# The first modulations of a diffusion block: pages of w_ada laid out in 4 KB rows, and VectorE's share turned and summed in one instruction

## Chip, cores and metric

The kernel runs on one core of a Trainium2 chip. The metric is device microseconds for one execution; a measurement gives the median of several runs. The profile is one further execution, taken by the hardware profiler.

## The reference

One layer of a diffusion backbone over 1024 latent tokens and 256 context tokens, 1024 channels wide, everything in float32. A conditioning vector sets shift, scale and gate of every sublayer, and the context has a vector of its own:

```python
mods   = jnp.split(jax.nn.silu(c) @ w_ada[layer] + b_ada[layer], N_MOD, axis=-1)            # N_MOD = 9
mods_c = jnp.split(jax.nn.silu(c_ctx)[None] @ w_ada[layer] + b_ada[layer], N_MOD, axis=-1)
h  = ffn_sublayer(h,  mods[0],   mods[1],   mods[2],   g_ffn1[layer], w_ffn1_in[layer], w_ffn1_out[layer])
hc = ffn_sublayer(hc, mods_c[0], mods_c[1], mods_c[2], g_ffn1[layer], w_ffn1_in[layer], w_ffn1_out[layer])
# ffn_sublayer: hn = rmsnorm(h, g) * (1 + scale) + shift; a, b = split(hn @ w_in); h + 0.5 * gate * ((silu(a) * b) @ w_out)
```

Behind it come a mixing layer, a second such sublayer and a norm. Only the first two modulations (m = 0, the shift, and m = 1, the scale) bear on the change: 2 x 1024 columns of w_ada, each a sum over 1024 channels, for two vectors (q = 0 for c, q = 1 for c_ctx).

## The kernel before

Channels lie on partitions, tokens on the free axis, so a modulation vector is a tile of 128 partitions by 8 blocks (index d). Products of weights run in float32 split into a high and a low float32r part: `split` copies the high part on ScalarE (L145) and subtracts it on VectorE (L146), and `mm3` (L182) multiplies high by high, high by low and low by high.

The kernel begins with the context's first feed-forward layer. Its input `hnc` needs the norm of the context and the modulations 0 and 1 for c_ctx. Their 2048 columns of w_ada are cut into four quarters of 256 columns (qt 0 to 3; two blocks d of both m). Quarters 0, 1 and 3 go to TensorE: `ada_page` (L844) loads a page of two channel blocks, each by a transfer of 256 KB whose rows are two pieces of 1 KB; `ada_rows` (L850) multiplies it with silu(c) and silu(c_ctx) as two stationary columns, so that the sums lie along the free axis of two partitions; `ada_copy` (L854) takes them to SBUF, `ada_flip` (L859) turns them onto partitions, and `ada_done` (L879, L887) adds the bias and makes the scale. Quarter 2 goes to VectorE: `side` multiplies and adds each page into two accumulators (L791, L793), `ada_red` transposes and reduces them (L797, L798), and `ada_side` adds the four groups of partitions through a product (L867) and eight small adds (L871).

`nct` is the context's norm: squares on ScalarE (L205, L208) and their sum on VectorE (L209), `rstd` (sums on TensorE L214, a short chain on VectorE, a diagonal L224, L225), `bcast` (L230), `scaled0` (L938). `mod0(d, ...)` makes blocks of hnc: an activation with scale and bias (L931) and a cast (L932) on ScalarE, the low part on POOL for even d and on VectorE for odd d (L934). `idle` runs small products on `junk` (L922).

TensorE, VectorE and ScalarE run in exactly the order in which this part is written, up to the end of the first weight pair (f = 0). In that pair the products of the first six channel blocks come first; `last0`, called inside it, flips quarter 3, makes blocks 6 and 7 of hnc and loads the third weight tile. All loads are issued by SP, in order. `W.load` brings a tile of w1i (512 KB, rows of 4 KB) and splits it. The page pool `hnp` has two tags, pg0 and pg1, of 8 slots of 4 KB each per partition; `fxpage` has 12.

## Time and profile before

| | |
|---|---|
| median of 3 runs | 2645.05 us (2644.9 to 2646.2) |
| the profiled execution | 2649.01 us, span 2647.2 us |
| TensorE busy | 2630.2 us, 99% of the span |
| VectorE busy | 1947.5 us, 74% |
| ScalarE busy | 1202.1 us, 45% |
| POOL busy | 75.3 us, 3% |
| bytes moved by DMA | 452.73 MB, mean 171 GB/s |

Busy time is what the profiler records for an engine's instructions. Matmuls are pipelined, so a busy TensorE is not one at its peak. A matmul of float32 operands shows as two passes. Times in the rows count from the span's start.

### The profile page before, as it was taken

The numbers are of one execution on the slowest core, as the hardware profiler recorded it, in microseconds if no ns is written. First come the engines' busy times: TensorE is split into PE (matmuls) and PEld (weight loads), VectorE is DVE, ScalarE is ACT, GpSimd is POOL, SyncE is SP. The second block draws the span as 40 slices with busy tenths as digits, with TensorE's granted clock in tenths as the row PEclk, the third lists the DMA queues.
The fourth block names the chain that finished last, engine by engine and source line by source line (L and its number), as shares of the span: only waits on it lengthen the run. The fifth ranks groups of instructions, "written<-read, shape, count | busy, mean of one in ns | idle before, by whom it ended". The sixth has DMA issues, their size and how long they took to land.

```text
span 2647.2 us, 35936 instructions
## 1 busy us (share of the span) xinstructions
PE 2630.2 (99%) x12904; PEld 2212.0 (84%) x12904; DVE 1947.5 (74%) x3490; ACT 1202.1 (45%) x2167; POOL 75.3 (3%) x158
## 2 busy tenths in 40 slices
PE   9999999999999999999999999999999999999998
PEld 6998888888889878888888888888888888888887
DVE  7988688687989646777674878777568766665855
ACT  5664444444347525564443454333256444344433
POOL 0000000000000000000000002221000000000000
PEclk9999999999999999999999999999999999999999
DMA  9833344368587122356653566547341333337644
GB/s 313 308 112 132 123 163 164 115 237 302 176 278 262 66 80 91 104 175 197 197 177 106 174 207 233 176 152 268 128 143 41 128 139 115 120 123 278 201 159 178
DMA packets 201234, 452.73 MB, mean 171 GB/s; under 512 B 20320, under 2 KB 54624, under 8 KB 201056
## 3 DMA queue, kind: packets, MB, share of 16 engines
q1 hardware_dynamic: 200624, 450.05, 50.2%
q8 instruction: 101, 1.65, 0.3%
q14 instruction: 77, 0.63, 0.1%
q10 hardware_dynamic: 432, 0.39, 0.0%
HBM read 329.11 MB, written 121.32 MB: 170 GB/s over the span
## 4 chain that ended last, share of the span: by engine, by line
PE 93%; DMA 3%; issue 2%; DVE 1%; ACT 1%; SPq 0%; POOL 0%; POOLq 0%; DVEq 0%; ACTq 0%
PE qa L411 18%; PE pq L1379 16%; PE po L535 14%; PE qb L411 14%; PE pt L1863 10%; PE pr L1298 6%; PE pa L182 2%; PE pc L1165 2%; PE pb L182 2%; PE pn L2018 2%; DMA adapg<-in_w_ada_dram 1%; PE pu L1699 1%; PE pkc L1358 1%; PE pn L2016 1%; PE pvc L1455 1%
## 5 line engine op out<-in xcount | busy, mean ns | idle before, releaser
L146 DVE TENSOR_TENSOR ring<-rawq,ring 128x512 fp32r<-128x512 f32 x408 | 281.0, 689 | 222.3 <-ACT ring L145 220.9
L535 PE MATMUL po<-gring,wring 128*128 128x512 f32 (+1 forms) x1896 | 423.5, 384 | 0.0
L535 PEld LDWEIGHTS po<-gring,wring 128*128 128x128 f32 x1896 | 349.4, 188 | 70.1
L145 ACT CAST ring<-rawq 128x512 fp32r<-128x512 f32 x408 | 253.5, 622 | 310.9 <-PE pq L1379 84.6
L411 PE MATMUL qa<-fc,ring 128*128 128x512 f32 x1056 | 252.3, 389 | 0.0
L411 PEld LDWEIGHTS qa<-fc,ring 128*128 128x128 f32 x1056 | 198.1, 188 | 41.5 <-DVE fc L146 0.4
L1379 PE MATMUL pq<-fc,ring 128*128 128x512 f32 x864 | 207.4, 392 | 1.8 <-DVE sg L1437 1.8
L145 ACT CAST wring<-rw 128x512 fp32r<-128x512 f32 x154 | 95.7, 623 | 219.3 <-PE po L535 191.2
L1379 PEld LDWEIGHTS pq<-fc,ring 128*128 128x128 f32 x864 | 161.4, 188 | 35.1 <-DVE sg L1437 2.2
L1863 PE MATMUL pt<-yp,ring 128*128 128x512 f32 x768 | 186.3, 396 | 0.0
L1863 PEld LDWEIGHTS pt<-yp,ring 128*128 128x128 f32 x768 | 144.2, 190 | 28.7
L146 DVE TENSOR_TENSOR wring<-rw,wring 128x512 fp32r<-128x512 f32 x154 | 105.7, 687 | 83.6 <-ACT wring L145 83.2
L1379 PE MATMUL pq<-fa,ring 128*128 128x512 f32 x576 | 141.9, 394 | 0.0
L1379 PE MATMUL pq<-fb,ring 128*128 128x512 f32 x576 | 136.8, 391 | 0.0
L411 PE MATMUL qa<-fa,ring 128*128 128x512 f32 x528 | 126.9, 390 | 0.0
L411 PE MATMUL qa<-fb,ring 128*128 128x512 f32 x528 | 126.5, 390 | 0.0
L411 PE MATMUL qb<-fb,ring 128*128 128x512 f32 x528 | 126.4, 389 | 0.0
L1379 PEld LDWEIGHTS pq<-fb,ring 128*128 128x128 f32 x576 | 107.5, 188 | 22.4 <-issue 0.2
L411 PE MATMUL qb<-fc,ring 128*128 128x512 f32 x528 | 126.2, 389 | 0.0
L411 PE MATMUL qb<-fa,ring 128*128 128x512 f32 x528 | 126.2, 389 | 0.0
L1379 PEld LDWEIGHTS pq<-fa,ring 128*128 128x128 f32 x576 | 106.9, 188 | 22.0 <-DVE ring L146 0.3
L793 DVE SCALAR_TENSOR_TENSOR adacc<-adapg,sc,adacc 128x512 f32<-128x512 f32 x154 | 111.9, 746 | 17.1 <-DMA adapg<-in_w_ada_dram 15.9
(366 smaller groups left out, 4641.3 us busy)
## 6 DMA issues: line engine op xcount, KB each, us to landing
adapg<-in_w_ada_dram SPq DMA_DIRECT2D x144, 256.0 KB, 3.6
fsp<-fhl SPq DMA_DIRECT2D x66, 512.0 KB, 2.7
gring<-fsp SPq DMA_DIRECT2D x66, 512.0 KB, 4.2
raw<-in_w1i_dram SPq DMA_DIRECT2D x44, 512.0 KB, 5.1
graw<-fsp SPq DMA_DIRECT2D x88, 256.0 KB, 3.4
rawq<-in_w1i_dram SPq DMA_DIRECT2D x38, 512.0 KB, 3.6
rawq<-in_w2i_dram SPq DMA_DIRECT2D x38, 512.0 KB, 3.5
fsp<-p SPq DMA_DIRECT2D x66, 256.0 KB, 2.1
```

Source lines behind the costliest of these rows:

```text
L145: hi = S.copy(hl[:, 0, :], src)
L146: return hi, V.tensor_sub(hl[:, 1, :], src, hl[:, 0, :].bitcast(F32))
L182: T.matmul(pt, x, y, start=first and i == 0, stop=i == n - 1, skip_group_check=True)
L411: T.matmul(pt, hl[:, x, sl], pages[p][k][:, y, :], start=first and i == 0, stop=i == 11, skip_group_check=not first)
L535: T.matmul(pt[:, cs], w[:, x, sl], g[:, y, cs], start=grp and kp == 0 and i == 0, stop=kp == NFP - 1 and i == 2, skip_group_check=not grp)
L793: eng.scalar_tensor_tensor(acc, pgt, sc2[:, q, k:k + 1], acc, ALU.mult, ALU.add)
L1165: T.matmul(pt, hl[d // 4][:, x, sl], g[:, y, :], start=f == 0 and d % 2 == 0 and i == 0, stop=f == NF - 1 and i == 2, skip_group_check=True)
L1298: T.matmul(self.pt[m], pg[:, x, sl], hl[:, y, :], start=first and k == 0 and i == 0, stop=k == 3 and i == 2, skip_group_check=not first)
L1358: T.matmul(self.cp[:, o:o + 256], hl[:, x, k * 128:(k + 1) * 128], hnc[kc][:, y, :], start=p == 1 and k == 0 and i == 0, stop=p in (2, 4) ...
L1379: T.matmul(pt, hl[:, x, k * 128:(k + 1) * 128], pg[k][:, y, :], start=first and k == 0 and i == 0, stop=k == 3 and i == 2, skip_group_chec ...
L1863: T.matmul(pt, hl[:, x, k * 128:(k + 1) * 128], pg[:, y, :], start=kh + k + i == 0, stop=kh == 1 and k == 3 and i == 2)
L2018: T.matmul(pn[:, 0:257], qi[:, c_, :], self.C[d][:, c_, :], start=False, stop=c_ == 1)
```

## The change

The first two modulations are cut into 16 units of one block d of one m. Eleven go to TensorE (four, four and three in the groups 0, 1 and 3), five to VectorE. TensorE's pages are laid out by the host so that a page is one transfer with rows of 4 KB (3 KB in group 3). VectorE's units are turned by the host: output channels on partitions, the 1024 input channels along the free axis. To multiply them, silu(c) and silu(c_ctx) are spread over all partitions (`spread`: 16 products on TensorE, four copies on ScalarE), and one instruction for each unit and vector, `tensor_tensor_reduce`, multiplies a page with the spread row and sums the 1024 products, beginning with the bias, straight into `mods`. The accumulators, transposes, reductions and the eight small adds go. The counts of `idle` change, hnc's pair 4, 5 is made ahead of pair 2, 3, and the rest of w_ada keeps its rows in an array of its own.

```diff
     def ada_load(page, m, hf, k):
         pgt = page()
-        o = m * 1024 + hf * 512
+        o = (m - 2) * 1024 + hf * 512
...
-    NQ = 4
-    QW = 1024 // NQ
-    QD = QW // 128
-    KP = 512 // QW
+    KP = 2
+    UNITS = {0: [(m, d) for m in range(2) for d in (0, 1)], 1: [(m, d) for m in range(2) for d in (2, 3)],
+             3: [(0, 6), (1, 6), (1, 7)]}
+    SIDE = [(0, 4), (1, 4), (0, 5), (1, 5), (0, 7)]
 
     def ada_page(qt, kp, tag):
-        pg = hnp.tile([128, KP, 2, QW], F32, name="adapg", tag=tag, bufs=8)
-        for i in range(KP):
-            src = a["w_ada"][kp * KP + i].rearrange("p (m c) -> p m c", m=9)[:, 0:2, qt * QW:(qt + 1) * QW]
-            nc.sync.dma_start(pg[:, i], src)
...
+        pg = hnp.tile([128, KP, len(UNITS[qt]) * 128], F32, name="adapg", tag=tag, bufs=8)
+        nc.sync.dma_start(pg.rearrange("p k c -> p (k c)"), a[f"w_ada{qt}"][kp])
...
+    def side_page(u):
+        pg = hnp.tile([128, 1024], F32, name="adaT", tag="pg0", bufs=8)
+        nc.sync.dma_start(pg, a["w_adaT"][u])
+        return pg
...
-    def ada_side(qt, reds):
...
-        for q, red in enumerate(reds):
-            T.matmul(p8[:, q * 16:q * 16 + 16], grp4, red[:, 0:16], start=True, stop=True)
-        for q in (1, 0):
-            for r in range(4):
-                sl = slice(32 * r, 32 * r + 32)
-                V.tensor_add(mods[sl, 0:2, q, cs],
-                             p8[sl, q * 16:q * 16 + 16].rearrange("p (m d r) -> p m d r", m=2, r=4)[:, :, :, r], bv[sl, 0:2, cs])
-            scale_mod(0, 1, q, "g_ffn1", cs)
...
         for q in (1, 0):
...
+            if qt == 3:
+                ab = ((slice(0, 2), 6, pc[:, q:q + 3:2]), (slice(1, 2), 7, pc[:, q + 4:q + 5]))
+                for ms, d, src in ab:
+                    V.tensor_add(mods[:, ms, q, d], src, bv[:, ms, d])
+                scale_mod(0, 1, q, "g_ffn1", slice(6, 8))
...
-    for qt, kp in ((2, 0), (0, 0), (0, 1), (2, 1), (0, 2), (0, 3), (2, 2), (1, 0), (1, 1), (2, 3), (1, 2), (1, 3),
-                   (3, 0), (3, 1), (3, 2), (3, 3)):
-        pgs[qt, kp] = ada_page(qt, kp, "pg1" if qt % 2 else "pg0")
-    idle(30)
...
+    for qt, kp in ((0, 0), (0, 1), (2, 0), (0, 2), (0, 3), (2, 1), (1, 0), (1, 1), (2, 2), (1, 2), (1, 3), (2, 3),
+                   (3, 0), (3, 1), (2, 4), (3, 2), (3, 3)):
...
+    scB = [fxpage("scB", F32, (128, 1024)) for _ in range(2)]
+    waste = fxpage("waste", F32, (128, 1024))
...
+    def spread():
+        for q in range(2):
+            for hf in range(2):
+                pt = sm_ps("psc")
+                for j in range(4):
+                    T.matmul(pt[:, j * 128:(j + 1) * 128], sc2[:, q, hf * 4 + j:hf * 4 + j + 1].to_broadcast([128, 128]), ident,
+                             start=True, stop=True)
+                yield lambda q=q, hf=hf, pt=pt: S.copy(scB[q][:, hf * 512:(hf + 1) * 512], pt)
+
+    def side(u, qs=(1, 0)):
+        m, d = SIDE[u]
+        for q in qs:
+            V.tensor_tensor_reduce(waste, adaT[u], scB[q], 1.0, vs_("b_ada")[:, m * 8 + d:m * 8 + d + 1], ALU.mult, ALU.add,
+                                   mods[:, m, q, d:d + 1])
+
+    idle(14)
+    copies = list(spread())
     for d in range(NKT):
         nct.sq(d)
-    side(0, pgs[2, 0])
+    for f in copies:
+        f()
+    idle(5)
     prs = {0: mm_ps("adr")}
     ada_rows(prs[0], pgs[0, 0], 0)
     nct.rstd()
-    ada_rows(prs[0], pgs[0, 1], 1)
-    idle(3)
-    side(1, pgs[2, 1])
-    ada_rows(prs[0], pgs[0, 2], 2)
+    for kp in (1, 2):
+        ada_rows(prs[0], pgs[0, kp], kp)
+    side(0)
     nct.bcast()
     ada_rows(prs[0], pgs[0, 3], 3)
-    row = ada_copy(prs[0])
     scaled0()
-    side(2, pgs[2, 2])
-    idle(4)
+    row = ada_copy(prs[0], 0)
+    prs[1] = mm_ps("adr")
+    ada_rows(prs[1], pgs[1, 0], 0)
+    side(1)
+    for q in (1, 0):
+        scale_mod(0, 1, q, "g_ffn1", slice(4, 5))
     pc = sm_ps("adc")
     ada_flip(pc, row)
     ada_done(0, pc)
     mod0(0, 1)
-    prs[1] = mm_ps("adr")
-    for kp in range(NKT // KP):
+    for kp in (1, 2, 3):
         ada_rows(prs[1], pgs[1, kp], kp)
-    row = ada_copy(prs[1])
-    side(3, pgs[2, 3])
-    reds = [cp.tile([128, 32], F32, name="adred", tag="adred", bufs=2) for _ in range(2)]
-    for acc, red in zip(sides, reds):
-        ada_red(acc, red, 0)
+    row = ada_copy(prs[1], 1)
+    side(2)
+    side(3)
+    for q in (1, 0):
+        scale_mod(0, 1, q, "g_ffn1", slice(5, 6))
+    mod0(4, 5)
     prs[3] = mm_ps("adr")
     ada_rows(prs[3], pgs[3, 0], 0)
     pc = sm_ps("adc")
     ada_flip(pc, row)
     ada_done(1, pc)
     mod0(2, 3)
-    ada_rows(prs[3], pgs[3, 1], 1)
-    ada_side(2, reds)
-    for kp in (2, 3):
+    side(4)
+    for kp in (1, 2, 3):
         ada_rows(prs[3], pgs[3, kp], kp)
     W.load()
-    mod0(4, 5)
-    row = ada_copy(prs[3])
+    row = ada_copy(prs[3], 3)
     W.load()
...
+    r["w_ada"] = np.ascontiguousarray(wada[:, 2048:]).reshape(8, 128, 7168)
+    unit = lambda m, d: wada[:, m * 1024 + d * 128:m * 1024 + d * 128 + 128]
...
+        r[f"w_ada{qt}"] = np.ascontiguousarray(w.reshape(4, 2, 128, -1).transpose(0, 2, 1, 3)).reshape(4, 128, -1)
+    r["w_adaT"] = np.ascontiguousarray(np.stack([unit(*u).T for u in ((0, 4), (1, 4), (0, 5), (1, 5), (0, 7))]))
```

## Rows read from the trace of the kernel before

**Rows 1.** Page, part 1: busy us, share of the span and instructions, by engine.
```profile
PE 2630.2 (99%) x12904; PEld 2212.0 (84%) x12904; DVE 1947.5 (74%) x3490; ACT 1202.1 (45%) x2167; POOL 75.3 (3%) x158
```

**Rows 2.** Stretches: length, busy (count) PE, PEld, DVE, ACT, POOL, clock, DMA, GB/s.
```profile
6.50:30.50 24.00, 23.38 (x95) 9.28 (x93) 20.19 (x52) 6.09 (x16) 0.73 (x1) 1.00 1.09 349
30.50:36.00 5.50, 5.50 (x22) 2.05 (x22) 3.48 (x17) 3.38 (x6) 0.72 (x1) 1.00 1.04 400
...
45.30:175.00 129.70, 129.70 (x1052) 128.27 (x1053) 117.83 (x178) 87.06 (x127) 0.00 (x0) 1.00 0.74 258
```

**Rows 3.** Tile adapg up to 60 us: issues on SP, and issue to landing.
```profile
L844 SPq DMA_DIRECT2D adapg<-in_w_ada_dram x32: 367/368/1020, 2.7 to 27.3; - x32
...
DMA to landing us min/median/max: 6.0/6.0/7.6
```

**Rows 4.** Order of time, VectorE (DVE), 10 to 46 us: start, length, instruction.
```profile
15.71 2.73 DVE L793 SCALAR_TENSOR_TENSOR adacc<-adapg,sc,adacc 128x512 f32<-128x512 f32 x4
18.36 2.73 DVE L938 TENSOR_TENSOR hc<-hc,rb 128x256 f32<-128x256 f32 x8
21.00 2.73 DVE L793 SCALAR_TENSOR_TENSOR adacc<-adapg,sc,adacc 128x512 f32<-128x512 f32 x4
23.66 0.15 DVE L879 TENSOR_TENSOR mods<-adc,vec 128x4 f32<-128x4 f32 x1
...
26.11 0.42 DVE L934 TENSOR_TENSOR hnc<-nt,hnc 128x256 fp32r<-128x256 f32 x1 [1.84 <-ACT hnc L932]
26.45 2.73 DVE L793 SCALAR_TENSOR_TENSOR adacc<-adapg,sc,adacc 128x512 f32<-128x512 f32 x4
...
31.78 0.15 DVE L879 TENSOR_TENSOR mods<-adc,vec 128x4 f32<-128x4 f32 x1
...
34.17 0.42 DVE L934 TENSOR_TENSOR hnc<-nt,hnc 128x256 fp32r<-128x256 f32 x1 [1.77 <-ACT hnc L932]
...
36.19 1.23 DVE L146 TENSOR_TENSOR hl<-raw,hl 128x1024 fp32r<-128x1024 f32 x1
```

**Rows 5.** Order of time, TensorE (PE), 0 to 50 us.
```profile
10.05 1.88 PE L850 MATMUL adr<-adapg,sc 128*2 128x512 f32 x4 [0.36 <-DMA adapg<-in_w_ada_dram]
11.86 0.61 PE L214 MATMUL p<-ones,acc 128*128 128x1 f32 x4
...
33.63 3.60 PE L850 MATMUL adr<-adapg,sc 128*2 128x512 f32 x8
37.16 2.49 PE L182 MATMUL pa<-hnc,hl 128*128 128x256 f32 x18
39.58 1.05 PE L859 MATMUL adc<-cst,adrow 2*128 2x2 f32 x8
```

**Rows 6.** Stretch of the junk matmuls (L922) alone: PE busy and passes.
```profile
4.70:9.40 4.70, 4.70 (x44) 4.70 (x43) 1.00 1.08 357
```

**Rows 7.** Order of time, ScalarE (ACT), 5 to 46 us.
```profile
14.71 0.69 ACT L224 ACTIVATE diag<-cst,rs_y 128x128 fp32r<-128x128 f32 x2 [5.70 <-DVE rs_y L770]
...
25.04 0.60 ACT L931 ACTIVATE nt<-hc,mods,smod 128x256 f32<-128x256 f32 x1
```

**Rows 8.** Groups by form, VectorE, whole span: count, busy us, mean ns.
```profile
L1468 DVE SCALAR_TENSOR_TENSOR cv<-pre,vec,cv 128x1023 f32<-128x1023 f32 x16 | 20.4, 1278 | 0.9 <-ACT cv L1467 0.9
...
L791 DVE TENSOR_SCALAR adacc<-adapg,sc 128x512 f32<-128x512 f32 x22 | 10.2, 479 | 0.0
...
L225 DVE SCALAR_TENSOR_TENSOR diag<-cst,rs_y,diag 128x128 fp32r<-128x128 f32 x32 | 9.6, 348 | 1.4 <-ACT diag L224 1.4
...
L1592 DVE TENSOR_TENSOR_SCAN bcz<-R,bcz 128x128 f32<-128x128 f32 x1 | 0.4, 426 | 0.1
```

**Rows 9.** Stretches around a gap of TensorE, columns as in rows 2.
```profile
1581.30:1583.90 2.60, 0.00 (x0) 0.00 (x0) 2.60 (x5) 2.60 (x6) 2.55 (x6) 1.00 0.88 280
...
1585.00:1588.50 3.50, 3.50 (x11) 2.82 (x10) 3.50 (x7) 2.02 (x5) 0.00 (x0) 0.51 1.01 361
1588.50:1592.00 3.50, 3.50 (x17) 2.85 (x17) 2.96 (x7) 2.22 (x5) 0.00 (x0) 1.00 1.01 350
```

## The prediction

> **What bounds the kernel now.** I read the page first: TensorE is busy for 99% of the span [rows 1]. The change lies wholly ahead of the first weight products, so next come the stretches by time: from 45.3 to 175 us TensorE works without a gap [rows 2]. The stretch before that is a lead-in, and a microsecond saved or lost at its end moves everything behind it by a microsecond, because TensorE has no slack later with which to make it good. The measure of the change is therefore when TensorE enters steady work, about 45.3 us now.

> Inside the lead-in two things run side by side. The pages of w_ada stream from about 6.5 to 30.5 us at 349 GB/s, and as soon as tiles with 4 KB rows follow, the rate is 400 GB/s [rows 2]. The last page is issued at 27.3 us and takes about 6.0 us to land, so 33.3 us [rows 3]. VectorE meanwhile goes through one list in program order [rows 4]: four passes of multiply-add (two at 15.71 to 21.00 and so on), the scaling of the context by its norm, the adds that finish each quarter's modulations, and every second low part of hnc. The low part of W's first tile ends that list at 36.19 + 1.23 = 37.42 us. TensorE's row products end just then: its last eight begin at 33.63 and the first product of the weights at 37.16 [rows 5]. So at 37.4 us three chains arrive almost together: pages, TensorE's rows, VectorE's list. A change that shortens two of them gains nothing if the third gets longer.

> **The pages.** The bytes stay the same: 16 units of 128 columns by 1024 rows, 8.39 MB. At 349 GB/s they take 24.0 us, at 400 GB/s 21.0 us [rows 2]: the last page lands 3 us earlier, near 30.3 us. SP issues 17 transfers where it issued 32, and is nowhere last. The ninth page of the pg0 group must wait until TensorE has read the first one, at 10.65 + 1.88 = 12.5 us [rows 5], before its turn comes; no transfer queues behind it for that.

> **TensorE's own list.** Out go 36 of the 74 junk passes, the 4 small products of p8 and a quarter of each of the 16 passes of the last rows (384 columns for 512). In come 32 passes of 128 columns that spread silu(c). A pass of that shape takes 4.7/44 = 0.11 us [rows 6]. Ahead of the first rows stand 28 + 32 + 10 = 70 such passes instead of 60, so they end 10 x 0.11 = 1.1 us later. The old ones were over at about 9.5 us, and the old rows then stood waiting for their page until 10.05 [rows 5]; the new rows can begin at 9.5 + 1.1 = 10.65, with their page there: +0.6 us. The norm's sums move from 11.86 to 12.46 us [rows 5], and with them all that VectorE does after them. From there: sums 0.61, 28 row passes at (37.16 - 33.63)/8 = 0.44, the broadcast's two passes at 0.14 (2.49/18, also of 256 columns), 16 passes of three quarters at 0.33, two flips at 1.05 [rows 5]: 12.46 + 0.61 + 12.32 + 0.28 + 5.28 + 2.10 = 33.1 us. The new list of TensorE is done 4 us earlier than before, and the last page, wanted at 31.8 us, is there. If the pages came no faster, the last would hold these rows until about 34.6 us, which, as the next part shows, would also cost nothing.

> **ScalarE's copies.** Four copies of 128x512 out of PSUM come in behind the squares. ScalarE takes 0.60 us for 256 columns, so at most 1.2 each and 4.8 for the four, and it sat idle for 5.70 us before 14.71 [rows 7]: hidden. Without that idle time they would delay the norm, and through it the list below, by up to 4.8 us.

> **VectorE's blocks.** Ten instructions of 1024 elements replace sixteen of 512, two transposes, two reductions and eight adds of 32 partitions. No such multiply-and-sum is in the trace. The nearest row has two f32 inputs, a pointer scalar and 1023 elements: 1.278 us [rows 8]. Below it bounds the one-input form, 0.479 us for 512 [rows 8], about 0.75 for 1024; two tensors are read here, and no two-input f32 row comes near that. Above it bounds the scan: 0.426 us for 128x128 where the ordinary form takes 0.348 [rows 8]; if those 0.078 us go with the elements, 1024 of them cost 0.62 more, 1.90 us. I take 1.28, and 1.30 from one to the next, because all ten write the same scratch page.

> Now the list, step by step, old times from [rows 4]. The first pair begins at 15.71 + 0.60 = 16.31 and ends at 18.91. The scaling takes 2.64 (18.36 to 21.00): 21.55. Second pair: 24.15. Two small scale steps, 0.15 as the row at 23.66 and the hand-over, 0.18 each: 24.51. The adds of the first quarter begin there (before: 23.66, now +0.85), and the first low part begins 2.45 later as before (23.66 to 26.11), since VectorE waits for ScalarE: 26.96, done at 27.30. Two more pairs, 5.20: 32.50. Here the order changes: hnc's pair 4, 5 stands ahead of pair 2, 3. ScalarE gets its scale about 0.28 us later, at 32.78, and needs 1.07 (25.04 to VectorE's 26.11) [rows 4, 7]: 33.85. VectorE stands idle for this, with everything behind it: the adds of the next quarter, the last pair of blocks, W's splits. (POOL's half of pair 4, 5 is issued earlier too, and has until 40 us; W's raw tile, behind the pages in SP's queue, lands 3 us earlier than it did and waits.) Low part: 34.19. Adds and wait for pair 2, 3, as before 31.78 to 34.17, 2.39: 36.58, done 36.92. Last pair of blocks: 39.52. Then W's first split, which began at 36.19: **+3.3 us**. The removed transposes, reductions and adds are in this sum already, since they stood where the last pairs stand now. What is late next: the third product of the weights needs that low part, so TensorE, ready at 33.1, does two products when ScalarE's cast is there (about 37.7 us) and then waits until 40.75. Behind it lie the flip of the last quarter (6 passes for 8, 1.05/8 each, -0.26) and an add more before its scale (+0.1), and so ScalarE's last pair, W's third tile and steady work: **+3.2 us** in sum.

> **TensorE's clock.** TensorE now has a hole of about 4.6 us and one of 2.8 us. [...] On the chain stand 16 products after the wait, at 2.49/18 = 0.14 us, 2.2 us, and the flip. Bounds: nothing, if the clock is back by 40.75; 2.6 us, if all of it runs at half. By the row's ratio, 2.2 x (17/11 - 1) = **+1.2 us**, which I take.

> Sum: 3.2 + 1.2 = +4.4 us. On the profiled execution's own time, 2649.01 us, that is 2653.4. The median of the runs, 2645.05, lies 4.0 us lower, a difference that I let stand as that of a profiled run; from it the forecast is **2649.4 us**. A measurement can tell about 0.2%, 5.3 us, from no change, so this counts as no change, on the slow side.

> **The rivals.** *A block costs two instructions* (slower). If the sum comes out through a second, short instruction, each block grows by about the smallest VectorE row, 0.15 us [rows 4]: ten times, all on the chain, +1.5: 2650.9. It is decided at 5.3 us: (5.3 - 4.4)/10 = 0.09 us per block, so from 1.39 us a block on the kernel is measurably slower. The margin is small. Nothing in the trace speaks for or against it. [...]

> *A block runs at the scan's pace* (slower): ten times 0.62, +6.2 us over the forecast, 2655.6. Only its likeness to a scan speaks for it, and the row has 128 elements alone, so the excess may as well be a fixed 0.08 us.

> *VectorE isn't last* (faster side). If a block takes only 0.75 us, the list shortens by 5.3 us, W's split begins at 34.2, the hole for the clock is gone: 3.2 - 5.3 = -2.1, 2643.0. With blocks for nothing, TensorE's 33.1 against 37.16 caps the gain at 4.1 us, 2641: the lead-in alone can't give a measurable gain.

> *The rest moves.* The scratch pages are free again before their slots are wanted, and the later reads of w_ada keep rows of 2 KB; a shifted order of transfers later on could add or take some microseconds either way.

> **Chances.** Forecast (block 1.2 to 1.39 us) 0.55, of which 0.06 beyond 5.3 us through the clock; two instructions 0.19, of which 0.13 beyond it; scan's pace 0.06; VectorE not last 0.16; the rest 0.04, half of it each way. Slower 0.06 + 0.13 + 0.06 + 0.02 = 0.27; faster 0.03 (the rest, and a hundredth of the fourth); no change 0.70. The range takes in the fast rival and the two-instruction one with the clock's upper bound (+1.4), and leaves out the scan: 2642.5 to 2652.5 us.

> **What would show it.** Right: pages done by about 30.5 us with the rate near 400; TensorE's rows over at 33 us and a hole behind them; blocks at 1.28 us; W's first split beginning at 39.5 us; a granted clock under 1.00 near 38 to 44 us; steady work about 4 us later. Wrong: blocks under 1 us, W's split before 36 us, a chain of waits that again runs through the pages, or a difference that arises after 50 us.

## The result, and the profile after

The changed kernel takes 2656.15 us (median of 6 runs, 2652.2 to 2659.1) where the kernel before takes 2645.89 beside it (6 runs, 2644.9 to 2650.2): a ratio of **1.0033, 95% interval 1.0023 to 1.0043**, or 6 to 11 us. It is slower by a third of a per cent, more than the 4.4 us of the forecast. The profiled execution took 2654.72 us, its span 2652.9.

Part 1 of the page of the kernel after: the totals hardly move [rows 1], so the answer lies in the order of things, not in the sums.

```profile
PE 2631.8 (99%) x12894; PEld 2217.4 (84%) x12894; DVE 1945.4 (73%) x3486; ACT 1204.1 (45%) x2171; POOL 74.9 (3%) x158
```

The kernel after in stretches (columns as in [rows 2]):

```profile
6.50:30.50 24.00, 24.00 (x107) 10.56 (x106) 16.72 (x48) 8.62 (x20) 1.98 (x2) 1.00 1.03 407
30.50:36.00 5.50, 3.35 (x11) 0.73 (x9) 3.92 (x11) 1.70 (x4) 0.45 (x1) 1.00 0.76 291
36.00:41.40 5.40, 0.80 (x2) 0.51 (x2) 4.09 (x7) 3.48 (x6) 0.72 (x1) 0.59 0.00 0
41.40:45.20 3.80, 3.77 (x17) 3.55 (x17) 1.71 (x2) 0.00 (x0) 0.00 (x0) 0.50 0.61 196
45.20:50.60 5.40, 5.40 (x26) 5.38 (x26) 1.72 (x9) 2.86 (x5) 0.73 (x1) 0.50 0.95 321
50.60:54.00 3.40, 3.22 (x27) 3.01 (x27) 2.56 (x3) 2.01 (x2) 0.00 (x0) 1.00 0.53 201
```

The pages do what was forecast: 407 GB/s for 349, and no transfer at all between 36.0 and 41.4 us. In that stretch TensorE works for 0.80 us of 5.40. The column of the granted clock is the surprise: 0.50 all the way from 41.4 to 50.6 us, while TensorE is busy for 9.17 of those 9.2 us. In [rows 9] it came back after 3.5 us.

Tile adapg, issues on SP and landing, answering [rows 3]: the last is issued at 18.9 us, so it lands by 29.5.

```profile
L842 SPq DMA_DIRECT2D adapg<-in_w_ada_dram x12: 328/328/504, 2.7 to 18.9; - x12
DMA to landing us min/median/max: 8.2/10.2/10.6
```

TensorE in order of time, answering [rows 5]:

```profile
29.82 4.03 PE L853 MATMUL adr<-adapg,sc 128*2 128x384 f32 x12
38.24 0.80 PE L182 MATMUL pa<-hnc,hl 128*128 128x256 f32 x2 [4.39 <-ACT hl L145]
41.43 3.78 PE L182 MATMUL pa<-hnc,hl 128*128 128x256 f32 x16 [2.38 <-DVE hl L146]
45.14 1.44 PE L863 MATMUL adc<-cst,adrow 2*128 2x2 f32 x6
46.51 4.21 PE L182 MATMUL pb<-hnc,hl 128*128 128x256 f32 x18
```

The rows are over at 33.85 us. Then come a hole of 4.39 us (ScalarE's cast of W's first tile, L145, stands behind its work for pair 2, 3), two products, and a second hole of 2.38 us until VectorE delivers W's low part (L146). Eighteen products of this shape took 2.49 us [rows 5]; those of the second tile now take 4.21.

VectorE in order of time, answering [rows 4]:

A block is two instructions: 1.28 us, and a read of the accumulator of 0.08. A second block starts 1.33 us after the first; an instruction of another kind starts together with the read, 1.21 us after. So a pair takes 2.54 us (17.10 to 19.64). The waits for ScalarE are all still there (0.98 and 1.78 us), and the last pair of blocks stands behind them.

The chain of waits of the kernel after, from 36 us, says the same from the other end: ScalarE's work for pair 2, 3, VectorE's low part, blocks, the split, and then nothing but TensorE.

```profile
37.28 0.42 DVE hnc L930
37.70 1.20 DVE waste L961
...
40.24 1.15 DVE hl L146
41.38 0.04 issue
41.43 3.78 PE pa L182 x16
45.21 1.37 PE adc L863 x6
46.58 4.14 PE pb L182 x18
```

Set beside the matmuls of the kernel before one by one, those of the kernel after are 7.33 us late when steady work begins. A stall of 0.28 us and the products around it add 0.5 near 90 us; from there the lag is 7.87 us up to 1190 us of the older kernel's time, within the 6 to 11 us of the timed runs. It then shrinks to 5.5 us by 2000, so the two profiled executions differ by only 5.7 us (2654.72 and 2649.01). Every other profile gains 1 to 2 us on that of before at the same place, 1196 us, so that step belongs to the execution of before. Below, *lag* means this: how much later than in the profile of before a kernel's steady work begins (46.07 us there).

### The profile page after: what moved, and what is told of

It reads as the page before. It is cut to its first block, busy times and chain, and to the rows that moved or that the text cites. A ratio compares the mean times of both kernels' runs of the same rounds, so it can differ in the third digit from the quotient of the medians.

```text
span 2652.9 us, 35897 instructions
## 1 busy us (share of the span) xinstructions
PE 2631.8 (99%) x12894; PEld 2217.4 (84%) x12894; DVE 1945.4 (73%) x3486; ACT 1204.1 (45%) x2171; POOL 74.9 (3%) x158
## 3 DMA queue, kind: packets, MB, share of 16 engines
q1 hardware_dynamic: 194368, 450.05, 49.8%
## 4 chain that ended last, share of the span: by engine, by line
PE 94%; DMA 2%; issue 2%; DVE 1%; ACT 1%; SPq 0%; POOL 0%; POOLq 0%; DVEq 0%; ACTq 0%
PE qa L411 18%; PE pq L1392 17%; PE po L535 15%; PE qb L411 14%; PE pt L1876 9%; PE pr L1311 5%; PE pb L182 2%; PE pc L1178 2%; PE pa L182 2%; PE pn L2031 2%; PE pu L1712 1%; PE pkc L1371 1%; PE pn L2029 1%; PE pvc L1468 1%; PE pu L1751 1%
## 5 line engine op out<-in xcount | busy, mean ns | idle before, releaser
L146 DVE TENSOR_TENSOR ring<-rawq,ring 128x512 fp32r<-128x512 f32 x408 | 281.7, 691 | 222.3 <-ACT ring L145 220.9
L145 ACT CAST ring<-rawq 128x512 fp32r<-128x512 f32 x408 | 253.4, 622 | 311.3 <-PE pq L1392 87.3
L411 PEld LDWEIGHTS qa<-fc,ring 128*128 128x128 f32 x1056 | 198.3, 188 | 41.4 <-DVE fc L146 0.4
L145 ACT CAST wring<-rw 128x512 fp32r<-128x512 f32 x154 | 95.6, 622 | 214.1 <-PE po L535 187.3
L146 DVE TENSOR_TENSOR wring<-rw,wring 128x512 fp32r<-128x512 f32 x154 | 106.2, 690 | 80.7 <-ACT wring L145 80.4
L411 PEld LDWEIGHTS qb<-fb,ring 128*128 128x128 f32 x528 | 99.1, 188 | 20.9 <-ACT fb L145 0.4
```

The costliest lines, as they stand in the source:

```text
L145: hi = S.copy(hl[:, 0, :], src)
L146: return hi, V.tensor_sub(hl[:, 1, :], src, hl[:, 0, :].bitcast(F32))
L411: T.matmul(pt, hl[:, x, sl], pages[p][k][:, y, :], start=first and i == 0, stop=i == 11, skip_group_check=not first)
```

## The experiments

The theory: VectorE's list ends later, TensorE meets a hole ahead of the first products, and the granted clock then halves. Its rivals: the wider pages, or the new order of hnc's pairs, cost the time. Ratios are to the kernel before, run on the same chip.

**e1_fill.** The changed kernel with TensorE kept busy behind its last rows.

```diff
         ada_rows(prs[3], pgs[3, kp], kp)
+    idle(32)
     W.load()
     row = ada_copy(prs[3], 3)
```

> The changed kernel with 32 junk products (64 passes at 0.11 us, 7.1 us) behind TensorE's last row products, so that TensorE has work nearly up to the wait for W's first low part (33.9 to 41.4 us in the changed kernel). Theory A (VectorE's list makes TensorE wait, and the idle time halves the granted clock, which then doubles what the 18 + 18 + 12 products of the first pair cost): the clock stays at 1.00 through the lead-in, the third product still begins near 41.5 us, the 18 products of pb take 2.4 us instead of 4.2, steady work begins near 49.8 us instead of 53.1, and the time falls by 3 to 4 us to some 4 us over the kernel before. Rival B (the clock falls for another reason, such as the row products with two stationary columns): the clock falls all the same, and nothing is gained. Rival C (the lead-in isn't the cause): steady work begins earlier, and the time stays.

Measured: 2650.38 us, 1.0016 (1.0007 to 1.0025); lag 2.62 us for 7.33; 1.11 of the difference is earlier sums of the norm (12.19 us for 13.30). TensorE in order of time:

```profile
32.66 7.41 PE L918 MATMUL junk<-ones 128*128 128x128 f32 x64
39.83 2.66 PE L182 MATMUL pa<-hnc,hl 128*128 128x256 f32 x18
```

The granted clock is 1.00 from 3.9 us to the kernel's last few microseconds, and a part of the loss is gone, though TensorE was given more work.

**e2_pages_only.** The kernel before, with each page as one transfer whose rows are 4 KB.

```diff
-        for i in range(KP):
-            src = a["w_ada"][kp * KP + i].rearrange("p (m c) -> p m c", m=9)[:, 0:2, qt * QW:(qt + 1) * QW]
-            nc.sync.dma_start(pg[:, i], src)
+        nc.sync.dma_start(pg.rearrange("p k m c -> p (k m c)"), a["w_adap"][qt, kp])
...
```

> The kernel before with only the layout of the pages changed: each page one transfer of 512 KB with rows of 4 KB, and VectorE's quarter multiplied and added as before. Theory A: the stream of pages is done about 3 us earlier (near 27.5 us instead of 30.5), TensorE's rows wait less, but VectorE's list sets W's first split, which was at 36.19 us and can move by a microsecond at most, so the time is the kernel before's within 1.5 us, rather faster. Rival D (the larger transfers cost, because a page is there only when all of its 512 KB are): later first rows, and a time 1 us or more above the kernel before.

Measured: 2646.95 us, 1.0001 (0.9992 to 1.0009); lag 0.18 us. In the stretches the rate is that of the changed kernel, 407 GB/s:

```profile
6.50:30.50 24.00, 24.00 (x103) 10.21 (x101) 20.13 (x51) 5.69 (x14) 0.72 (x1) 1.00 1.03 407
```

Nothing comes of it. TensorE waits for no page any more, and works without a gap until 37.44 us; then it waits for VectorE's low part, for 0.20 us:

```profile
37.64 2.18 PE L182 MATMUL pa<-hnc,hl 128*128 128x256 f32 x16 [0.20 <-DVE hl L146]
```

With the pages out of the way, TensorE's own list and VectorE's end together, and neither is earlier than before.

**e3_rows_1k.** The changed kernel with pages and turned blocks moved in pieces of 1 KB.

```diff
-        nc.sync.dma_start(pg.rearrange("p k c -> p (k c)"), a[f"w_ada{qt}"][kp])
+        nc.sync.dma_start(pg.rearrange("p k c -> p (k c)").rearrange("p (s c) -> p s c", c=256),
+                          a[f"w_ada{qt}"][kp].rearrange("s p c -> p s c"))
...
-        nc.sync.dma_start(pg, a["w_adaT"][u])
+        nc.sync.dma_start(pg.rearrange("p (s c) -> p s c", c=256), a["w_adaT"][u].rearrange("s p c -> p s c"))
...
```

> The changed kernel with its pages and turned blocks stored so that each transfer reads pieces of 1 KB, as before the change; all else is the changed kernel. Theory A: the stream falls back to about 350 GB/s and ends near 30.5 us; TensorE's rows end up to 2 us later, inside the hole; VectorE's list and the time stay as in the changed kernel within 1 us, so the faster pages bring the changed kernel nothing. Rival D: the time gets better without the 4 KB rows. Rival E (the pages do pay): 2 to 3 us slower than the changed kernel.

Measured: 2654.63 us, 1.0035 (1.0021 to 1.0049); lag 6.03 us, and 7.9 after the stall near 90 us. The rate is 349 GB/s again and the time that of the changed kernel: its 3 us of earlier pages bring nothing here. From the norm's sums to the third product it is 28.12 us (12.43 to 40.55), in the changed kernel 28.13.

**e4_order.** The changed kernel with hnc's pair 4, 5 back behind W's first load.

```diff
         scale_mod(0, 1, q, "g_ffn1", slice(5, 6))
-    mod0(4, 5)
...
     W.load()
+    mod0(4, 5)
     row = ada_copy(prs[3], 3)
```

> The changed kernel with hnc's pair 4, 5 made where it was made before the change, behind W's first load, instead of ahead of pair 2, 3. Theory A: VectorE loses its wait of 0.98 us ahead of that low part, and the 0.4 us of the low part, so W's first split begins near 38.8 us instead of 40.15 and the third product near 40.1 instead of 41.4; the hole is shorter but the clock still falls. The time gets 1 to 1.5 us better, or up to 3 if the clock comes back one step earlier. Rival B: no change.

Measured: 2652.35 us, 1.0025 (1.0016 to 1.0034); lag 5.14 us. W's first split begins at 37.39 us (40.15; 38.8 expected), so the move of that pair was a part of the list's cost: 2.76 us, less the 1.01 by which the sums were earlier in this execution, 1.75. The holes are 2.64 and 3.21 us, and the clock still halves, from 38.3 to 48.5 us.

**f3_hole and f4_hole_fill.** The disputed cost by itself: the kernel before, with nothing of the change, and six adds ahead of W's first split; f4 has junk products in the hole.

```diff
         ada_rows(prs[3], pgs[3, kp], kp)
+    idle(16)                      # f4 only
+    hole = t2("hole")
+    for _ in range(6):
+        V.tensor_add(hole, sides[0], sides[1])
     W.load()
```

> The kernel before, with six adds of 128x512 on VectorE (about 0.6 us each) put ahead of W's first split; nothing of the change is in it. This measures by itself what a list that ends 3.7 us later costs. Theory (the late list opens a hole on TensorE and the granted clock halves after it): W's split near 39.9 us, clock 0.5 for some 10 us behind it, steady work later by 3.7 us of list and 2 to 4 us of clock: 5.5 to 7.5 us, a ratio of 1.0021 to 1.0029. Rival (the rest of the change's loss comes from the blocks, the pages or the moved pairs and the clock costs 1.2 us as forecast): 3.7 to 5 us, 1.0014 to 1.0019.

> As f3_hole, with 16 junk products on TensorE behind its last rows, so that it isn't idle while VectorE's list ends. Theory: the clock stays at 1.00 and only the list is left, 3.5 to 4 us later than the kernel before, a ratio of 1.0013 to 1.0016; the difference to f3_hole is the price of the clock. Rival: the time is that of f3_hole, since junk products save nothing.

Measured: f3 2653.58 us, 1.0027 (1.0017 to 1.0038), lag 5.62; f4 2652.67 us, 1.0020 (1.0011 to 1.0029), lag 5.05. The timed runs don't separate the two. The traces do. TensorE in f3, and f3's stretch behind the hole:

```profile
41.67 3.60 PE L182 MATMUL pa<-hnc,hl 128*128 128x256 f32 x16 [4.48 <-DVE hl L146]
```

```profile
41.90:45.30 3.40, 3.40 (x17) 3.17 (x16) 2.39 (x4) 0.00 (x0) 0.00 (x0) 0.50 0.68 195
45.40:50.00 4.60, 4.60 (x36) 4.34 (x37) 1.29 (x6) 3.10 (x6) 0.74 (x1) 1.00 0.98 313
```

and in f4:

```profile
42.59 2.17 PE L182 MATMUL pa<-hnc,hl 128*128 128x256 f32 x16 [1.26 <-DVE hl L146]
```

The same 16 products take 3.60 us behind the hole and 2.17 with the hole filled: 1.43 us for the clock, which was half for 3.4 us and not for the expected 10. The adds took 0.77 us each, so the list came 4.6 us later where 3.7 was expected. The sums came at 11.42 us in f3 and 12.38 in f4 (11.86 before); without that, the lags are 6.06 and 4.53 us, and their difference, 1.53, is again the clock's price. One hole of 4.5 us thus costs about 1.5 us, close to the forecast's 1.2. It doesn't explain the changed kernel's loss.

**g1_after_again, g2_first_hole, g3_second_hole.** What is different there: two holes. g1 is the changed kernel again; g2 fills the first hole, g3 the second (with a hook in `mm3` that isn't shown).

```diff
         ada_rows(prs[3], pgs[3, kp], kp)
+    idle(18)                              # g2 only
     W.load()
+    between.append(lambda: idle(9))       # g3 only: run behind the second product
     row = ada_copy(prs[3], 3)
```

> The changed kernel once more, for a second look at its lead-in. Its first profile showed a half clock for 13.7 us, from 36.97 to 50.62; the kernel with one added hole of 4.5 us showed 3.4 us. If the long spell belongs to the two holes of this kernel, it is seen again, 10 us or more; if it was this one execution, the spell is 3 to 7 us and steady work begins 1 to 3 us earlier than 53.4 us.

> The changed kernel with 18 junk products behind TensorE's last rows: the first hole (4.4 us, up to the first product) is filled, the second (2.4 us, up to the third) stays open. If each hole adds to the time at half clock, a spell of at most 3.4 us is left behind the second hole, and steady work begins between that with both filled (48.7) and the changed kernel's (53.4), near 50 us: a ratio of 1.0016 to 1.0022. Rival: the second hole alone is what matters, since it lies right ahead of the products on the chain: the spell and the time stay as in the changed kernel.

> The changed kernel with 9 junk products between the second and third product of the weights: the second hole is filled, the first stays open. If each hole adds, the clock falls in the first hole, near 37 us, and is back earlier than 50.6 us, near 44 to 47: steady work near 50 to 51.5 us, a ratio of 1.0018 to 1.0026. Rival: the first hole alone sets the spell, and it stays 10 us or more with a time like the changed kernel's.

Measured: g1 one run, 2655.57 us, lag 7.63: half clock from 37.39 to 51.04 us, 13.7 us as in the first profile, so it isn't that one execution's. g2 2655.68 us, 1.0029 (1.0020 to 1.0038), lag 3.94. g3 2652.55 us, 1.0018 (1.0009 to 1.0027), lag 6.09. TensorE and the stretch of the second hole in g2:

```profile
33.54 4.29 PE L918 MATMUL junk<-ones 128*128 128x128 f32 x36
37.99 0.51 PE L182 MATMUL pa<-hnc,hl 128*128 128x256 f32 x2 [0.17 <-ACT hl L145]
41.18 2.16 PE L182 MATMUL pa<-hnc,hl 128*128 128x256 f32 x16 [2.68 <-DVE hl L146]
```

```profile
38.50:41.20 2.70, 0.02 (x1) 0.03 (x1) 2.66 (x6) 0.76 (x1) 0.00 (x0) 1.00 0.00 0
41.20:46.00 4.80, 4.80 (x38) 4.65 (x39) 2.85 (x9) 0.91 (x2) 0.00 (x0) 1.00 0.75 213
```

and in g3:

```profile
38.40 0.79 PE L184 MATMUL pa<-hnc,hl 128*128 128x256 f32 x2 [4.38 <-ACT hl L145]
38.99 4.04 PE L922 MATMUL junk<-ones 128*128 128x128 f32 x18
```

With the first hole filled, the second (2.68 us) doesn't touch the clock in this profile. With the first open, the clock falls in it, at 37.33 us, and is back at 44.15: half for 6.8 us instead of 13.7. So neither hole sets the price alone: the clock comes down in the first, and with the second open it stays down while the products on the chain run. (g3's junk products ran at half clock too and ended 1.1 us after the low part was ready, so its lag is that much too long.) The list of g2 is the changed kernel's with the clock at 1.00: its sums came 0.24 us earlier, so the same list has a lag of 4.18 us there and 7.33 in the changed kernel. **The clock's price is 3.2 us** by this pair of profiles; e1, read in the same way, gives 3.6 (7.33 less 2.62 and 1.11).

g2's time is the study's misfit: expected 1.0016 to 1.0022, measured 1.0029, which the timed runs don't tell from the changed kernel's 1.0033. So the price of 3.2 us is a reading of traces. That the clock was half for a shorter time in g2's timed runs too is seen in their granted clock over the whole span, 0.997 in the median for 0.995 in the changed kernel. In g2's profile the lead-in's gain is there at 50 us, but it loses 0.9 us near 90, 1.4 at 620 and 1.7 at 1742 us, where the clock was half for 3.4 us. Such steps, of a few tenths to 2 us and of either sign, are in all the profiles, mostly at the same few places behind 600 us. No run here tried them. In all other kernels that were timed, the lag at 100 us lies in the interval of the ratio.

**f1_best, f2_best_1k, g4_best_fill.** If the list is the bound, the blocks can be used against it: they need no work of ScalarE, so they can stand where VectorE waits for it. ScalarE's half of `mod0` (`mod_hi`) goes ahead of a pair of blocks and VectorE's half (`mod_lo`) behind it; the head has fewer junk products. f2 is f1 with pieces of 1 KB as in e3; g4 is f1 with 12 junk products for 5 behind the last rows.

```diff
-    idle(14)
+    idle(8)
...
-    idle(5)
...
-    mod0(0, 1)
+    mod_hi(0, 1, 4)
+    side(2)
+    mod_lo(0, 1)
...
-    side(2)
     side(3)
...
-    mod0(4, 5)
+    mod_hi(5)
+    mod_lo(4)
...
-    mod0(2, 3)
+    mod_hi(2, 3)
     side(4)
+    mod_lo(5, 2, 3)
...
         ada_rows(prs[3], pgs[3, kp], kp)
+    idle(5)                       # g4: 12
     W.load()
```

> Theory: the only thing wrong with the change is that VectorE's list became the last chain. So this version takes the list's own waste out: the head has 6 junk products and the 5 ahead of the rows fewer (the sums about 1.2 us earlier), hnc's pairs are made in two steps (ScalarE's high parts first, the low parts on VectorE after a pair of blocks), so that VectorE works on blocks while it used to wait for ScalarE, and 5 junk products stand behind TensorE's last rows. Worked out: sums near 11.0, W's first split near 33.7, third product near 35 us (37.5 in the kernel before), clock 1.00 throughout, steady work about 2.5 us earlier than in the kernel before: 2643 to 2645, a ratio near 0.999. If VectorE's list was not what held the lead-in (rival: pages or TensorE's rows did), the third product stays at 37 us or later and the ratio at 1.000 or above.

> As f1_best, with the pages again in pieces of 1 KB. If the wider rows pay once VectorE's list is no longer last, the last page lands near 33.4 instead of near 30.5 us, TensorE's last rows end near 34.6 instead of 32, and steady work comes up to 1 us later than in f1_best: a difference at the edge of what can be measured, seen in the trace alone. If the wider rows never pay, the steady work of both begins within 0.2 us.

> f1_best with 12 junk products instead of 5 behind TensorE's last rows. In f1_best the clock fell to half from 35.70 to 39.12 us, and the 16 products behind the third took 3.48 us instead of 2.16. Filled: clock 1.00, third product near 35.3 as there, steady work 1.3 us earlier, near 43.8 (46.1 in the kernel before): 2644.5 to 2646 beside 2647, a ratio of 0.999 to 0.9995. If the clock falls all the same, it is 45.2 and no change.

Measured: f1 2648.28 us, 0.9999 (0.9990 to 1.0008), lag -0.89; f2 2647.53 us, 0.9996 (0.9987 to 1.0005), lag -1.57; **g4 2642.79 us, 0.9987 (0.9978 to 0.9995), lag -2.76**. VectorE in g4:

```profile
22.64 0.15 DVE L876 TENSOR_TENSOR mods<-adc,vec 128x4 f32<-128x4 f32 x1
22.83 0.16 DVE L883 SCALAR_TENSOR_TENSOR smod<-mods,vec 128x2 f32<-128x2 f32 x1
22.91 1.28 DVE L969 CUSTOM_DVE_ANT_0 waste<-adaT,scB,vec 128x1024 f32<-128x1024 f32 x1
...
33.68 2.35 DVE L146 TENSOR_TENSOR hl<-raw,hl 128x1024 fp32r<-128x1024 f32 x2
```

The block follows the adds at once, where the changed kernel waited for ScalarE; from 14.5 to 36 us VectorE has no wait at all. W's split begins at 33.68 us instead of 40.15, of which 2.6 us are earlier sums. TensorE in f1, and then in g4:

```profile
33.69 0.50 PE L182 MATMUL pa<-hnc,hl 128*128 128x256 f32 x2 [0.79 <-ACT hl L145]
35.31 3.48 PE L182 MATMUL pa<-hnc,hl 128*128 128x256 f32 x16 [1.12 <-DVE hl L146]
```

```profile
33.86 0.48 PE L182 MATMUL pa<-hnc,hl 128*128 128x256 f32 x2
34.94 2.17 PE L182 MATMUL pa<-hnc,hl 128*128 128x256 f32 x16 [0.60 <-DVE hl L146]
```

f1 got its list, but not the 2643 to 2645 us that were expected: the clock fell at 35.70 us for 3.4 us and took 1.3 back. In g4, with seven junk products more, it stayed at 1.00. g4 beats the kernel before by 0.13%, which 11 runs beside 27 just tell from none. f2's steady work begins 0.68 us earlier than f1's, not later: its rows end later, so that a wait of 0.43 us is left, and the clock stayed at 1.00. Beside g4, where the clock stayed too, it begins 1.19 us later. Of this 0.92 are the sums, and the rows ahead of them had to wait for their page until 9.77 us (until 9.23 in f1, with wide rows; in g4 they began at 8.85 without a wait). So the pages of 1 KB cost between 0.3 and 1.2 us here, and one execution of each doesn't say where between.

## Why the prediction was wrong

The forecast was +4.4 us and no measurable change; steady work began 7.3 us later in the trace, and the runs took 6 to 11 us more. The direction, the place and the mechanism (VectorE's late list, the hole, the fall of the clock) were right; a loss beyond 5.3 us through the clock had been given a chance of 0.06. **The step that failed is the clock's term**, "By the row's ratio, 2.2 x (17/11 - 1) = +1.2 us", with its upper bound of 2.6 us "if all of it runs at half": it measured 3.2 us.

Of the 2.9 us by which steady work came later than forecast, the clock's term is 2.0, the later sums 0.8 and the list 0.1. The stall near 90 us adds 0.5, and the kernel before was itself 0.8 us slower beside the changed one than in the runs that the forecast starts from. Of the 6.75 us between 2649.4 and 2656.15 some 2.5 are left without a cause; the changed kernel's runs lie 7 us apart.

- *The clock: 3.2 us for 1.2.* The text put 16 products at half clock, and the flip with them in its bound; its ratio, 17/11 = 1.55, is that of the passes in two stretches of 3.50 us in [rows 9], at a granted clock of 1.00 and of 0.51. At half clock stood those 16 (3.78 us for 2.16, a ratio of 1.75), the flip (1.44 for 0.82) and also the second tile's 18 products (4.21 for 2.40, each against g2): 4.0 us, of which 0.9 is made good in the waits behind. The bound left the second tile out; in [rows 9], with one gap, the clock was back after 3.5 us. f3 shows that for one hole a price of that size holds (1.5 us); g2 and g3 show that two holes in a row don't simply add.
- *VectorE's list.* Sums to W's first split were forecast as 39.52 - 12.46 = 27.06 us and took 40.15 - 13.30 = 26.85. The lag that is left in g2, at the changed kernel's sums, is 4.18 us; less the 0.84 us by which the sums came later than forecast, 3.34, for a forecast of 3.2. A block that ran beside POOL (1.62 us for 1.28, see the last section) is in it, which the text had not foreseen.
- *The sums: 13.30 for 12.46.* The forecast took the opening as in the profile of before. There a pass of the opening junk products takes 0.21 us up to 4.6 us (17 in 3.60) and 0.11 behind 4.7 us [rows 6]; the record of the granted clock begins between the two, at 4.68 us, with 1.00. That the clock was about half ahead of it, and rose there, is read from the passes: no record shows it. In this sense it rose at 6.25 us here, at 6.67 in g1 and at 3.91 in e1, with the same products ahead of it; the sums then came at 13.30, 13.51 and 12.19. That is 0.48 us of sums for each us of clock in these three profiles. With the 4.68 us of the kernel before, the sums would lie at 12.19 + 0.48 x 0.77 = 12.56, near the forecast, and the other 0.7 us belongs to this execution.
- *The blocks.* 1.28 us each, 2.54 a pair for the forecast's 2.60. The rival of two instructions was right in its fact, with 10 blocks and 10 reads in the trace, and wrong in its price: of the read's 0.08 us only some 0.05 lie on the chain (1.33 us from block to block for 1.28), and none where another kind of instruction follows (read and scaling both start at 19.64 us). No row of before showed such a read, so its 0.15 us a block and its chance of 0.19 were the author's estimates. The rivals of the scan's pace (1.90 us) and of a block under 1 us fall; that the scan's 2655.6 us lies near the measured 2656.15 is chance.
- *The pages.* Done by 29.5 us at 407 GB/s (30.3 and 400 forecast), and worth nothing, as forecast: e2 and e3.
- *ScalarE's copies* were hidden, as forecast. *The rest moves*: 0.5 us near 90 us here, and steps of a few tenths to 2 us later, both ways.

What stays open: why the clock falls in f1 after two short holes (0.79 and 1.12 us) and not in g2 after one of 2.68; whether it is the number of holes or where they lie in time that makes the spell long, since g2 and g3 have one profile each; and the steps late in the kernel.

## What to carry to other kernels

The faster instruction didn't help here, where its engine waits in program order for another one (VectorE for ScalarE, 0.98 and 1.78 us): look for the waits in the list, and put the work that depends on nobody into them (g4: the same blocks, and W's split 3.8 us sooner after the sums by the order of the list). Price a hole ahead of TensorE's work as the hole plus the work behind it at half clock, all of it that could be touched (16 products took 3.78 us for 2.16 here), and expect that two holes close together can cost more than each alone (3.2 us of clock for 4.39 and 2.38 us here, 1.5 for one of 4.48 in f3, none for one of 2.68 in g2). When the hole itself can't be closed, junk products in it can keep the clock up: it was 1.00 in the profiles of e1, f4, g2 and g4. What that brings is near the edge of what timed runs can tell: e1 was faster than the changed kernel, by it and by its earlier sums; g4 against f1 is at that edge, and f4 against f3 and g2 against the changed kernel aren't told apart.

## What the runs showed of the hardware

- The granted clock came back 9.2 us after TensorE had resumed without a gap (41.43 to 50.62 us; 9.4 us in g1, 41.62 to 51.04), and 3.7 us after it in f3 (41.67 to 45.32). In e3 and e4 it was half for 10.2 us.
- A hole of 2.68 us left the clock at 1.00 in g2, while in f1 a fall at 35.70 us followed 1.91 us of idling in two pieces, between 32.9 and 35.3 us.
- The time at which the clock first rises, read as above, differs from execution to execution, from 3.9 to 6.7 us, with TensorE working from 0.99 us each time, and moves the norm's sums by 1.3 us: more than several of the edits do.
- A multiply-and-sum of 128x1024 in f32 takes 1.28 us, the same as the two-input row of 1023 elements [rows 8].
- One block in ten took 1.62 us, in every profile with blocks but e4's. It is the one that begins while POOL makes the low part of a block of hnc. In the changed kernel POOL's instruction took 1.70 us there, and 0.72 where VectorE stood waiting:

```profile
26.52 0.72 POOL L930 TENSOR_TENSOR hnc<-nt,hnc 128x256 fp32r<-128x256 f32 x1 [25.55 <-ACT hnc L928]
29.25 1.70 POOL L930 TENSOR_TENSOR hnc<-nt,hnc 128x256 fp32r<-128x256 f32 x1 [2.00 <-ACT hnc L928]
```

In e4, where pair 4, 5 had moved, all ten blocks took 1.28, and W's first split, which then began while POOL worked, took 1.74 for 1.23 [rows 4]. In the changed kernel the block begun at 29.08 us, 0.17 ahead of POOL's instruction, took 1.29. So the instruction that VectorE began while POOL worked took 0.34 us more in the changed kernel and 0.51 more in e4, and POOL's beside the blocks 0.98 more; why, no run shows. An order of VectorE's list has also to be read beside POOL's.
